# Padding the weight buffers and the halves of h in an encoder trunk, so that their SBUF addresses are staggered

## Chip, cores and metric

One core of one Trainium2 chip runs the whole program in a single launch. The metric is the device time of one execution in microseconds (us), lower is better. The kernel before takes 1731.49 us (median of 3 runs, 1730.62 to 1733.04).

## What is computed

A two-layer encoder trunk on x of 512 positions by 1024 channels, in float32. Cut to what matters:

```python
for l in range(DEPTH):                                   # 2 layers
    mod = jax.nn.silu(c) @ w_ada[l] + b_ada[l]           # shift, scale, gate, twice
    h = layer_norm(x) * (1.0 + scale1) + shift1
    proj = h @ w_in[l]                                   # 1024 x 7168: q, k, v of 3 groups, pooling, 2 gates
    att = ...                                            # dilated band attention, 3 groups, 8 heads of 64
    y_att = att.reshape(B, S, ATT_WIDTH) @ w_att_out[l]
    pooled = ...                                         # centred pooling, mixed per group, scaled
    y_pool = pooled @ w_pool_out[l]
    merged = jax.nn.sigmoid(gate_att) * y_att + jax.nn.sigmoid(gate_pool) * y_pool
    x = layer_norm(ALPHA * x + (1.0 + gate1) * (merged @ w_o[l]), ln1_g[l], ln1_b[l])
    h2 = layer_norm(x) * (1.0 + scale2) + shift2
    a_, b_ = jnp.split(h2 @ w_ffn_in[l], 2, axis=-1)     # 1024 x 5632
    x = layer_norm(ALPHA * x + (1.0 + gate2) * ((jax.nn.silu(a_) * b_) @ w_ffn_out[l]), ln2_g[l], ln2_b[l])
```

## The kernel before

Positions and channels are cut into tiles of 128. Every large product is done in three float32r matmuls: both factors are split into a rounded part (hi) and a remainder (lo), and `mm3` (L237) adds hi·hi, hi·lo and lo·hi into one PSUM bank (L239, L240, L241). `proj` (L243) calls it for the eight 128-channel steps of h: the stationary operand is a 128x128 slice of a weight tile, the moving operand 512 columns (all positions) of h.

The weights come as chunks of 128x1024 (512 KB) by DMA from the SP queue into `raw` buffers, and `split` (L197) makes hi and lo of each: ACT rounds, DVE or POOL subtracts. `prefetch` (L86) walks the list of chunks ahead of use; by the list, hi and lo go either into buffers of the tag `w` (8 of 4,096 bytes in each partition) or into buffers of the tag `g` (23 of 4,096 bytes), which also hold activations, attention operands and weight tiles that stay. The tag `h` has two buffers of 16,384 bytes: each is one half of h, four channel tiles with hi and lo of 512 positions each (`new_h`, L267). `h(k)` (L270) is tile k, a pair of 512-column rows.

The stages of a layer, in program order: `values` (L381, matmuls of L389, where h is stationary and a weight row moving), pooling, q and k with attention in between, `gates` and `merge` (the second matmul group there has pooled or attended tiles of `g` moving against `w`), then `tail` (L764) for the product with w_o; `ffn_in` (L864, the first tiles in two halves of 256 columns, some of them from `g`); and `tail` again for w_ffn_out. In `tail` the matmuls (L775) have 128 columns of a `g` tile stationary and a 512-column half of a weight row moving, from `w` for most and from `g` for resident weights; each weight row is used by six matmuls for each tile of positions.

A pool places its tags one after the other in a partition. In values of 4 bytes, the built program before has the eight `w` buffers 1,024 apart, the two halves of h behind them 4,096 apart, and all ten start 232 values past a multiple of 512; the `g` buffers start 56 past one. Weight slices start at multiples of 128 in their buffer. So the difference between a moving row of h and a stationary slice of `w` is always a multiple of 128; that between a moving row of `w` and a stationary slice of `g` is 48 (modulo 128), and that between a moving tile of `g` and a slice of `w` is 80 (modulo 128).

DMAs that the POOL engine issues (activations, rows of constants, small exchanges for attention) use a scratch area of SBUF, 16,384 bytes of each partition at address 0.

Of the kernel before, what the change touches and what calls it, by code (L numbers as in the profile page):

```python
# [13 lines left out]
F32R = mybir.dt.float32r  # L14
# [3 lines left out]
D = 1024  # L18
S = 512
# [9 lines left out]
P = 128  # L29
# [11 lines left out]
NW = 8  # L41
# [7 lines left out]
class Net:  # L49
# [38 lines left out]
    def prefetch(self, loads, splits, scales=None):  # L88
        n = len(self.plan)
        scales = max(splits, scales or splits)  # L90
        loads = max(loads, scales)
        info = lambda i: (self.plan[i] + (None,))[2]
        for i in range(min(n, self.pos + loads)):
            if i not in self.raws and i not in self.ready:
                self.raws[i] = self.chunk(self.plan[i][0])
        for i in range(min(n, self.pos + scales)):
            if i in self.raws and i not in self.scaled and info(i) is not None and info(i) >= 0:
                assert not self.ada
                self.scaled.add(i)
                self.nc.gpsimd.tensor_mul(self.raws[i], self.raws[i], self.gate[info(i)][0])  # L100
        for i in range(min(n, self.pos + splits)):
            if i not in self.ready:
                raw = self.raws.pop(i)
                if self.plan[i][1] == "w":
                    hi, lo = (self.t("w", [P, D], F32R, NW) for _ in range(2))
                else:
                    hi, lo = self.g([P, D], F32R), self.g([P, D], F32R)
                self.split(hi, lo, raw, info(i) == -1)
                self.ready[i] = (hi, lo)
# [155 lines left out]
        return r  # L265

    def new_h(self):  # L267
        self.hA = [self.t("h", [P, 4, 2, S], F32R, 2) for _ in range(2)]

    def h(self, k):  # L270
        return self.hA[k // 4][:, k % 4]
# [749 lines left out]

# [11 lines left out]
```

## Time and profile before

| what | value |
|---|---|
| median of 3 runs | 1731.49 us |
| lowest and highest run | 1730.62 and 1733.04 us |
| profiled execution, first to last instruction (span) | 1732.1 us |
| the same execution in the view of cores | 1732.1 us, mean granted TensorE clock 0.994 |
| TensorE (PE) busy | 1688.3 us, 97%, 8162 matmuls |
| DVE, ACT, POOL busy | 965.5, 658.7, 351.1 us |
| share of PE in the chain that ended last | 90% |

The page tells of one profiled execution. Of PE it says when a matmul starts; ends are modelled and overlap the next start, so the pace is read from starts. PEld is the load of the stationary operand, one for each matmul. A view of groups gives, behind the count, the busy time, the mean duration of one in ns, and the idle time in front of them with what ended it.

### The profile page before, as it was taken

The page shows a single profiled execution, that of the slowest core. Times are in us where ns is not written, and L with a number is a line of the kernel's source. Part 1 is how long each engine was busy: PE and PEld are TensorE (multiplying, and loading weights), DVE is VectorE, ACT ScalarE, POOL GpSimd, SP SyncE. Part 2 cuts the span into 40 slices and gives each one's busy share as a digit, 9 for nine tenths or more (in the row PEclk, how much of TensorE's full clock was granted, in tenths as well). Part 3 has the DMA queues.
Part 4 walks back from the last instruction along what each step waited for, and adds up shares of the span by engine and source line. Part 5 has one row for each costly group of instructions (what it writes and reads, how often), then busy time and mean ns, then how long its engine had stood idle before and what let it go on. Part 6 is the DMA issues. An engine that isn't in the chain of part 4 may idle for free.

```text
span 1732.1 us, 21129 instructions
## 1 busy us (share of the span) xinstructions
PE 1688.3 (97%) x8162; PEld 1384.0 (80%) x8162; DVE 965.5 (56%) x1628; ACT 658.7 (38%) x1110; POOL 351.1 (20%) x317
## 2 busy tenths in 40 slices
PE   7899999999989999999999999999999999999998
PEld 5687788888779888888878887878887888888886
DVE  8657677545685554333473676764367844333435
ACT  4246444633443222221352554446234422222212
POOL 4301221002340000255330021120032400004540
PEclk9999999999999999999999999999999999999999
DMA  7524444332532555332522254452325344322331
GB/s 273 203 73 166 157 136 138 109 113 81 195 110 96 190 195 176 111 108 96 184 110 79 83 173 134 143 162 86 98 98 182 110 146 146 97 98 97 106 138 49
DMA packets 63799, 227.20 MB, mean 131 GB/s; under 512 B 7681, under 2 KB 8097, under 8 KB 63698
## 3 DMA queue, kind: packets, MB, share of 16 engines
q1 hardware_dynamic: 55296, 199.25, 33.9%
q0 software_dynamic: 8400, 26.59, 4.8%
q8 instruction: 64, 1.05, 0.3%
q14 instruction: 37, 0.30, 0.1%
q10 hardware_dynamic: 2, 0.00, 0.0%
HBM read 217.28 MB, written 8.54 MB: 130 GB/s over the span
## 4 chain that ended last, share of the span: by engine, by line
PE 90%; DVE 6%; ACT 2%; issue 1%; DMA 0%; POOL 0%; DVEq 0%
PE mm L239 21%; PE mm L241 20%; PE mm L240 20%; PE mm L775 8%; PE pt L775 5%; PE s L775 4%; PE mm L607 2%; PE mm L389 1%; DVE raw L205 1%; PE pt L389 1%; PE s L542 1%; PE s L541 1%; PE pt L573 1%; DVE nt L260 1%; DVE rs L264 1%
## 5 line engine op out<-in xcount | busy, mean ns | idle before, releaser
L239 PE MATMUL mm<-h,w 128*128 128x512 f32 (+1 forms) x1440 | 560.6, 389 | 0.0
L241 PE MATMUL mm<-h,w 128*128 128x512 f32 (+1 forms) x1440 | 554.6, 385 | 0.0
L240 PE MATMUL mm<-h,w 128*128 128x512 f32 (+1 forms) x1440 | 553.7, 385 | 0.0
L199 DVE TENSOR_TENSOR w<-raw,w 128x1024 fp32r<-128x1024 f32 x238 | 309.8, 1316 | 188.5 <-ACT w L198 188.5
L198 ACT CAST w<-raw 128x1024 fp32r<-128x1024 f32 x254 | 259.8, 1044 | 168.4 <-PE mm L775 141.7
L239 PEld LDWEIGHTS mm<-h,w 128*128 128x128 f32 x1440 | 270.6, 188 | 57.0 <-issue 3.8
L241 PEld LDWEIGHTS mm<-h,w 128*128 128x128 f32 x1440 | 270.6, 188 | 55.4
L240 PEld LDWEIGHTS mm<-h,w 128*128 128x128 f32 x1440 | 270.8, 188 | 52.4
L100 POOL TENSOR_TENSOR raw<-raw,g 128x1024 f32<-128x1024 f32 x60 | 158.2, 2648 | 375.0 <-DMA raw<-w_ffn_out 221.4
L198 ACT CAST g<-g 128x512 fp32r<-128x512 f32 x76 | 47.2, 621 | 336.7 <-DVE g L871 217.0
L775 PE MATMUL mm<-w,g 128*128 128x512 f32 x600 | 147.2, 395 | 0.0
L871 DVE TENSOR_TENSOR g<-g,mm 128x512 f32<-128x512 f32 x42 | 28.9, 688 | 211.4 <-PE mm L241 198.8
L775 PEld LDWEIGHTS mm<-w,g 128*128 128x128 f32 x600 | 112.6, 188 | 27.1
L205 DVE SCALAR_TENSOR_TENSOR raw<-raw,silc 128x1024 f32<-128x1024 f32 x96 | 132.2, 1384 | 1.6 <-DMA raw<-w_ada 1.6
L199 DVE TENSOR_TENSOR g<-g,g 128x512 fp32r<-128x512 f32 x76 | 61.9, 815 | 70.8 <-ACT g L198 70.8
L775 PE MATMUL s<-w,g 128*128 128x512 f32 x300 | 78.9, 403 | 2.1 <-ACT w L198 1.3
L775 PE MATMUL pt<-w,g 128*128 128x512 f32 x300 | 76.3, 395 | 0.0
L775 PEld LDWEIGHTS s<-w,g 128*128 128x128 f32 x300 | 57.5, 193 | 17.1 <-ACT w L198 1.8
L775 PEld LDWEIGHTS pt<-w,g 128*128 128x128 f32 x300 | 56.4, 188 | 13.6
L232 POOL DMA_DIRECT2D dg<-gr x4 | 2.1, 536 | 290.2 <-DVE gr L230 290.2
L473 POOL CAST kp<-kp 64x640 fp32r<-64x640 f32 x8 | 10.9, 1368 | 235.0 <-ACT kp L465 235.0
L870 ACT ACTIVATE g<-mm 128x512 f32<-128x512 f32 x42 | 25.2, 600 | 84.6 <-PE mm L241 84.6
(229 smaller groups left out, 2085.6 us busy)
## 6 DMA issues: line engine op xcount, KB each, us to landing
raw<-w_in SPq DMA_DIRECT2D x112, 512.0 KB, 3.3
raw<-w_ada SPq DMA_DIRECT2D x96, 512.0 KB, 4.3
raw<-w_ffn_in SPq DMA_DIRECT2D x88, 512.0 KB, 3.3
raw<-w_ffn_out SPq DMA_DIRECT2D x44, 512.0 KB, 3.2
raw<-w_o SPq DMA_DIRECT2D x16, 512.0 KB, 4.2
xs<-g POOLq DMA_DIRECT2D x12, 512.0 KB, 2.9
g<-xs POOLq DMA_DIRECT2D x12, 512.0 KB, 5.9
g<-d POOLq DMA_DIRECT2D x16, 256.0 KB, 5.6
```

Source lines behind the costliest of these rows:

```text
L100: self.nc.gpsimd.tensor_mul(self.raws[i], self.raws[i], self.gate[info(i)][0])
L198: self.nc.scalar.copy(dst_hi, src)
L199: (self.nc.gpsimd if pool else self.nc.vector).tensor_sub(dst_lo, src, dst_hi.bitcast(F32))
L205: self.nc.vector.scalar_tensor_tensor(raw, raw, 1.0, self.silc, op0=ALU.mult, op1=ALU.mult, accum_out=self.mod[:, l, m : m + 1])
L239: mm(out, lhsT=whi, rhs=xhi, start=first, stop=False)
L240: mm(out, lhsT=whi, rhs=xlo, start=False, stop=False)
L241: mm(out, lhsT=wlo, rhs=xhi, start=False, stop=last)
L389: nc.tensor.matmul(pv[p, g], lhsT=hh[:, hi, tk], rhs=w[k][wi][:, c], start=k == 0 and i == 0, stop=k == KD - 1 and i == 2)
L607: nc.tensor.matmul(o, lhsT=v, rhs=rhs, start=b == 0, stop=b == 1)
L775: mm(acc[t][hf], lhsT=src[k][:, part, tk], rhs=wx[:, hf * S : hf * S + S], start=k == 0 and part == 0 and wi == 0, stop=k == K - 1 and par ...
L870: nc.scalar.activation(tmp[:, 0], pa, AF.Silu)
L871: nc.vector.tensor_mul(tmp[:, 1], tmp[:, 0], pb)
```

## The change

Every `w` buffer is 8 values (32 bytes) longer, and the program uses the first 1,024 of it as before. Every half of h is 64 values (256 bytes) longer, and the program uses the first 4,096. The scratch area for the DMAs of POOL goes from 16,384 to 8,192 bytes. Together the ten buffers take 768 bytes more of each partition.

```diff
@@ prefetch
-                    hi, lo = (self.t("w", [P, D], F32R, NW) for _ in range(2))
+                    hi, lo = (self.t("w", [P, D + 8], F32R, NW)[:, 0:D] for _ in range(2))
@@ new_h
-        self.hA = [self.t("h", [P, 4, 2, S], F32R, 2) for _ in range(2)]
+        self.hA = [
+            self.t("h", [P, 8 * S + 64], F32R, 2)[:, 0 : 8 * S].rearrange("p (k e s) -> p k e s", k=4, e=2)
+            for _ in range(2)
+        ]
@@ kernel
-    nc = bacc.Bacc("TRN2", target_bir_lowering=False, num_devices=1)
+    nc = bacc.Bacc("TRN2", target_bir_lowering=False, num_devices=1, dynamic_dma_scratch_size=8192)
```

No instruction is added, removed or moved on any engine: each engine's list is the same, line by line, but for addresses. In the built program of the change the `w` buffers start 232, 240, 248, ... 288 values past a multiple of 512, the halves of h 296 and 360 past one, the `g` buffers 56 past one as before. The difference between a moving row of h and a stationary slice of `w` now takes, modulo 128, the sixteen values 0, 8, 16, ... 120 instead of 0 alone, in nearly equal numbers, by which buffer a chunk happens to get; `w` moving against `g` takes 48, 56, ... 104 instead of 48; `g` moving against `w` takes 24, 32, 48, ... 80 instead of 80.

## Rows read from the trace of the kernel before

**Rows 1.** The page: span and busy time of the engines.
```profile
span 1732.1 us, 21129 instructions
PE 1688.3 (97%) x8162; PEld 1384.0 (80%) x8162; DVE 965.5 (56%) x1628; ACT 658.7 (38%) x1110; POOL 351.1 (20%) x317
PEclk9999999999999999999999999999999999999999
```
**Rows 2.** The page: shares of the chain that ended last, by engine.
```profile
PE 90%; DVE 6%; ACT 2%; issue 1%; DMA 0%; POOL 0%; DVEq 0%
```
**Rows 3.** Groups by shape (line, engine, operation, names, shapes, count | busy us, mean ns | idle before).
```profile
L239 PE MATMUL mm<-h,w 128*128 128x512 f32 x1376 | 542.5, 394 | 0.0
L241 PE MATMUL mm<-h,w 128*128 128x512 f32 x1376 | 536.5, 390 | 0.0
L240 PE MATMUL mm<-h,w 128*128 128x512 f32 x1376 | 535.6, 389 | 0.0
L775 PE MATMUL mm<-w,g 128*128 128x512 f32 x600 | 147.2, 395 | 0.0
L775 PE MATMUL s<-w,g 128*128 128x512 f32 x300 | 78.9, 403 | 2.1 <-ACT w L198 1.3 <-DVE w L199 0.7
L775 PE MATMUL pt<-w,g 128*128 128x512 f32 x300 | 76.3, 395 | 0.0
L239 PE MATMUL mm<-g,w 128*128 128x512 f32 x128 | 50.5, 395 | 0.0
L239 PE MATMUL pt<-h,w 128*128 128x256 f32 x64 | 18.7, 292 | 0.0
```
**Rows 4.** Timeline of PE near 300 us (start, duration, line): h against w.
```profile
299.82 0.39 PE L241 MATMUL mm<-h,w 128*128 128x512 f32 x1
...
302.54 0.39 PE L241 MATMUL mm<-h,w 128*128 128x512 f32 x1
```
**Rows 5.** Timeline of the weight loads near 300 us.
```profile
299.82 0.19 PEld L239 LDWEIGHTS mm<-h,w 128*128 128x128 f32 x1
300.05 0.19 PEld L240 LDWEIGHTS mm<-h,w 128*128 128x128 f32 x1
```
**Rows 6.** Timeline of PE near 382 us: g against w.
```profile
381.79 0.39 PE L241 MATMUL mm<-g,w 128*128 128x512 f32 x1
...
383.86 0.39 PE L241 MATMUL mm<-g,w 128*128 128x512 f32 x1
```
**Rows 7.** Timeline of PE near 1713 us, in the last tail.
```profile
1712.71 2.96 PE L775 MATMUL mm<-w,g 128*128 128x512 f32 x12
1715.51 1.54 PE L775 MATMUL mm<-g,g 128*128 128x512 f32 x6
1716.89 2.49 PE L775 MATMUL mm<-w,g 128*128 128x512 f32 x10
```
**Rows 8.** Timeline of PE near 530 us: 256 columns of h against w.
```profile
529.26 0.28 PE L240 MATMUL pt<-h,w 128*128 128x256 f32 x1
...
530.94 0.28 PE L239 MATMUL pt<-h,w 128*128 128x256 f32 x1
```
**Rows 9.** Timeline of PE near 540 us: 256 columns of h against g.
```profile
539.91 0.28 PE L239 MATMUL mm<-h,g 128*128 128x256 f32 x1
...
541.44 0.28 PE L240 MATMUL mm<-h,g 128*128 128x256 f32 x1
```
**Rows 10.** Timeline of PE near 1373 us: 256 columns of h against g.
```profile
1373.16 0.28 PE L241 MATMUL mm<-h,g 128*128 128x256 f32 x1
...
1374.97 0.28 PE L239 MATMUL mm<-h,g 128*128 128x256 f32 x1
```
**Rows 11.** DMA issues (engine, count, KB each, us to landing) and the software queue.
```profile
q0 software_dynamic: 8400, 26.59, 4.8%
xs<-g POOLq DMA_DIRECT2D x12, 512.0 KB, 2.9
g<-xs POOLq DMA_DIRECT2D x12, 512.0 KB, 5.9
g<-d POOLq DMA_DIRECT2D x16, 256.0 KB, 5.6
```
**Rows 12.** Waits of PE (who waited for whom: us in total, times, longest).
```profile
PE mm L389 <- ACT h L375: 11.8, 7, 2.4
PE s L280 <- ACT g L838: 6.1, 4, 2.8
PE pt L240 <- DVE h L853: 5.4, 2, 2.9
```

## The prediction, made before the changed kernel was run

> **What bounds the kernel now.** [...] The chain that ended last is PE for 90% of its length, with DMA and POOL at 0% [rows 2], and the longest waits of PE come to 11.8, 6.1 and 5.4 us in total [rows 12]. So the time is the number of matmuls times their pace, and the change can matter only through that pace: it adds and moves no instruction. Next come the groups by shape. Three lines, L239 to L241, hold 4,128 matmuls of 512 columns of h against a slice of `w`, with no idle time before them [rows 3]; in L775 another 1,200 have a row of `w` moving against a slice of `g` [rows 3].
>
> Their durations (389 to 403 ns) are no pace, since they overlap. The pace is read from starts in the timeline. Of h against `w`, twelve steps take 2.72 us, 226.7 ns each [rows 4]; in 256 columns, fourteen steps take 1.68 us, 120.0 ns each [rows 8]. The difference, 106.7 ns for 256 columns, makes 213.3 ns for 512, so 13.3 ns of each matmul do not grow with its width. The load of the next stationary slice starts with the matmul, at 299.82 in both views [rows 4, 5]: two reads of SBUF run side by side, and what they cost each other is the question here.
>
> Whether their addresses matter can be seen before the change, because the trace has other differences. With 80 (modulo 128), `g` against `w`, in the same three lines and the same order, nine steps take 2.07 us, 230.0 ns [rows 6]. With 48, `w` against `g` in L775, twelve take 2.80 us, 233.3 ns; just behind it the same line with both from `g`, difference 0, takes 1.38 us for six, 230.0 ns [rows 7]. In 256 columns, 48 (h against `g`) takes 1.53 us for 13 steps, 117.7 ns [rows 9], and in another place 1.81 us for 16 steps, 113.1 ns [rows 10], both below the 120.0 of difference 0. So the 13.3 ns become 16.7 (230.0 less 213.3) or 20.0 (233.3 less 213.3) in wide matmuls, and 11.0 or 6.4 (117.7 or 113.1 less 106.7) in narrow ones. The address pair goes with the pace, by a few ns, to both sides.
>
> **The change, part by part.** The times below are made against the profiled execution, 1732.1 us, which stands 0.6 us above the median of 1731.49; sums are added to the median.
>
> *h against `w`, 512 columns: 4,128 matmuls.* Their difference goes from 0 to sixteen values, only one of which is 0 and only two of which (48 and 80) are in this trace at all. I bound the mean pace from the nearest rows. Upper end: all at the 230.0 of `g` against `w`, the same lines, width and order, +3.3 ns, +13.6 us. Lower end: the 256-column rows, -2.3 ns (117.7 against 120.0), -9.5 us; the lowest narrow row would be -6.9 ns, -28.5 us. I take half of the upper end, +1.65 ns or +6.8 us: the wide rows are nearest in form, and both of them with another difference than 0 lie above 226.7; but some of the sixteen may be as good as 0, so not all of them pay. Besides, the difference now changes with each hi and lo buffer, so a run no longer has one fixed difference to settle at.
>
> *`w` against `g` in the tails: 1,200 matmuls.* They sit at the highest pace of the wide rows, 233.3, and keep their 48 in about one of eight. Bounds: -3.3 ns (the 230.0 of the same line with difference 0), -4.0 us; and 0. I take the middle, -2.0 us.
>
> *256 columns of h against `w`: 384 matmuls* (six groups of 64 like the one shown) [rows 3]. Bounds -2.3 and 0 ns; the middle, -0.4 us.
>
> *`g` against `w` (384, three groups of 128 like the one shown [rows 3]) and `values` (384 in L389).* Some of their differences change. They run between 226.7 and 233.3 already, so I take 0 and keep 2.5 us (3.3 ns times 768) to each side.
>
> *ACT and DVE write, DMA fills.* `raw` buffers, which the DMAs write, keep their size; hi and lo are written at starts that are multiples of 32 bytes as before. I cost this at 0: ACT and DVE are busy for 38% and 56% [rows 1]. If that cover went, PE would wait for h or w, as it does now for 5.4 us [rows 12].
>
> *Half the scratch.* The software queue moves 8,400 packets in the whole run, and its transfers land 2.9 to 5.9 us after their issue [rows 11]. The trace does not show how full the scratch is. Below: nothing can be gained. Above: if each of the 12 loads of x in `g<-xs` waited for one earlier landing, 12 times 5.9 us, 71 us, of which POOL and DMA have none on the chain now [rows 2]. The issuing engine is idle for four fifths of the time, and each load stands a whole tail ahead of its use, so I take 0, and up to 3 us in the range.
>
> Sum: 6.8 - 2.0 - 0.4 = +4.4 us, 1731.5 + 4.4 = 1735.9, forecast **1736 us**, 0.26% slower. About 0.2% (3.5 us) is what a measurement of this kernel can tell from no change.
>
> **Rivals.** *The staggered addresses read past each other (faster).* For: both narrow rows with difference 48 are below that with 0; half of the new differences are odd multiples of 8, of which no wide matmul of this trace has one, and the 13.3 ns that do not grow with the width are there to be won. Against: no wide row here is below 226.7 for long. It decides from the point where the mean of the sixteen is under 226.7. At -2.3 ns for 4,128 and -4.0 us in the tails it gives 1731.5 - 9.5 - 4.0 = 1718 us; at the lowest narrow row, 1731.5 - 28.5 - 4.0 = 1699. [...]
>
> *All sixteen cost what the tails cost (slower by more).* 233.3 for 4,128 matmuls: 6.6 ns each, +27.2 us, and the tails stay as they are: 1759 us. For: it is the widest sample of a difference other than 0. Against: the rows of `g` against `w` are at 230.0.
>
> *The address pair is not what sets the pace (no change).* The rows with other differences are also other places of the program with other operands, other PSUM banks and other order, and in L775 the pace with difference 0 (230.0) is that of `g` against `w`. Then padding does nothing: 1731 to 1732 us. [...]
>
> **How the numbers follow.** Chances: the forecast (a little slower, 1735 to 1748) 0.36; all at the tails' pace or above 1748 0.11; faster, 1718 or below and up to 1728, 0.35; nothing, 0.18. The first two make slower 0.47. The range goes from 1715 (the faster case at 1718, less the 2.5 us for the two small groups) to 1750 (13.6 + 2.5 + 3 us above the median: all at 230.0, the small groups and the scratch at their upper ends); the case at 1759 and the lowest narrow row, together under 2 in 10, are left out. The forecast's own range is 1735 to 1748.
>
> **What would show it.** In the profile after, the instruction counts, and the waits of PE, should stand as they are. The pace of h against `w`, read from starts, should differ from place to place, with some pairs of buffers at about 226.7 and others at 230 or more, mean near 228.3; the tails' rows should fall from 233.3 towards 231.7. If the mean of h against `w` is under 226.7, or single places show 220 or less, the forecast is wrong and the first rival right; if it is 226.7 everywhere, the third. If POOL's DMA issues take longer, or PE waits for h in the tails for more than the 5.4 us [rows 12], the scratch has a price that I put at 0.

## The result and the profile after

The changed kernel takes 1749.88 us (median of 4 runs, 1746.73 to 1752.90), the kernel before 1731.05 us in the same comparison: 18.8 us more, a ratio of 1.0101 with a 95% interval of 1.0083 to 1.0120. It is slower, 0.1 us inside the upper end of the range (1750; two of the four runs lie above it) and well above the 1736 that was forecast.

The page of the changed kernel, the lines that answer to [rows 1, 2]:

```profile
span 1751.1 us, 21129 instructions
PE 1706.1 (97%) x8162; PEld 1382.5 (79%) x8162; DVE 962.3 (55%) x1628; ACT 658.8 (38%) x1110; POOL 352.0 (20%) x317
PE 90%; DVE 6%; ACT 2%; issue 1%; DMA 0%; POOL 0%; DVEq 0%
```

The counts and the chain are as before; PE is busy 17.8 us longer, the other engines as long as before to within 3.2 us. The waits of PE in the changed kernel (us in total, times, longest), which answer to [rows 12]:

```profile
PE mm L392 <- ACT h L378: 10.1, 6, 2.4
PE s L283 <- ACT g L841: 6.5, 4, 3.0
PE pt L240 <- DVE h L856: 5.7, 2, 2.9
```

These three come to 22.3 us, those of [rows 12] to 23.3; all waits of PE in the view come to 37.2 us, before to 35.8. So waits hold at most 1.4 of the 18.8 us, and the time went into the matmuls themselves. The groups by shape, which answer to [rows 3] (lines below L273 have moved by 3):

```profile
L239 PE MATMUL mm<-h,w 128*128 128x512 f32 x1376 | 548.3, 398 | 0.0
L240 PE MATMUL mm<-h,w 128*128 128x512 f32 x1376 | 543.4, 395 | 0.0
L241 PE MATMUL mm<-h,w 128*128 128x512 f32 x1376 | 543.1, 395 | 0.0
L778 PE MATMUL mm<-w,g 128*128 128x512 f32 x600 | 146.3, 394 | 0.0
L778 PE MATMUL s<-w,g 128*128 128x512 f32 x300 | 77.3, 397 | 1.7 <-ACT w L198 1.0 <-DVE w L199 0.8
L778 PE MATMUL pt<-w,g 128*128 128x512 f32 x300 | 75.9, 394 | 0.0
```

The three groups of h against `w` have together 20.2 us more busy time, the three of the tails 2.9 us less. Starts say the same more exactly. Near 303 us of the changed kernel:

```profile
302.60 0.40 PE L240 MATMUL mm<-h,w 128*128 128x512 f32 x1
...
305.66 0.40 PE L241 MATMUL mm<-h,w 128*128 128x512 f32 x1
```

That is thirteen steps in 3.06 us, 235.4 ns each, where [rows 4] have 226.7. This is one of the slowest places; the mean is below. In the last tail, beside [rows 7]:

```profile
1728.96 5.74 PE L778 MATMUL mm<-w,g 128*128 128x512 f32 x24
1734.54 1.55 PE L778 MATMUL mm<-g,g 128*128 128x512 f32 x6
```

24 steps of `w` against `g` take 5.58 us, 232.5 ns, below the 233.3 of before. Over the whole trace the mean step of h against `w` (each start to the next one, 4,064 pairs with no step over 280 ns in either trace) goes from 227.5 to 232.6 ns, that of the tails from 233.3 to 231.7, that of `g` against `w` from 230.5 to 232.1. All steps of h against `w` together, longer ones with them, sum to 20.9 us more, those of the tails to 3.3 us less, `g` against `w` to 0.6 us more.

### The profile page after: what moved, and what is told of

The parts are those of the page before. It is cut to its first block, busy times and chain, and to the rows that moved or that the text cites. A ratio compares the mean times of both kernels' runs of the same rounds, so it can differ in the third digit from the quotient of the medians.

```text
span 1751.1 us, 21129 instructions
## 1 busy us (share of the span) xinstructions
PE 1706.1 (97%) x8162; PEld 1382.5 (79%) x8162; DVE 962.3 (55%) x1628; ACT 658.8 (38%) x1110; POOL 352.0 (20%) x317
## 4 chain that ended last, share of the span: by engine, by line
PE 90%; DVE 6%; ACT 2%; issue 1%; DMA 0%; POOL 0%; DVEq 0%
PE mm L239 21%; PE mm L240 21%; PE mm L241 21%; PE mm L778 8%; PE pt L778 4%; PE s L778 4%; PE mm L610 2%; PE mm L392 1%; DVE raw L205 1%; PE pt L392 1%; PE s L545 1%; PE s L544 1%; PE pt L576 1%; DVE nt L260 1%; DVE rs L264 1%
## 5 line engine op out<-in xcount | busy, mean ns | idle before, releaser
L239 PE MATMUL mm<-h,w 128*128 128x512 f32 (+1 forms) x1440 | 566.2, 393 | 0.0
L240 PE MATMUL mm<-h,w 128*128 128x512 f32 (+1 forms) x1440 | 561.4, 390 | 0.0
L241 PE MATMUL mm<-h,w 128*128 128x512 f32 (+1 forms) x1440 | 561.1, 390 | 0.0
L199 DVE TENSOR_TENSOR w<-raw,w 128x1024 fp32r<-128x1024 f32 x238 | 304.9, 1295 | 190.0 <-ACT w L198 190.0
```

The lines of the kernel that those rows point to most:

```text
L199: (self.nc.gpsimd if pool else self.nc.vector).tensor_sub(dst_lo, src, dst_hi.bitcast(F32))
L239: mm(out, lhsT=whi, rhs=xhi, start=first, stop=False)
L240: mm(out, lhsT=whi, rhs=xlo, start=False, stop=False)
L241: mm(out, lhsT=wlo, rhs=xhi, start=False, stop=last)
```

## The experiments

Two theories stood against each other from the start. **A:** each difference between the moving and the stationary address has its own price. **B:** a fixed difference settles at a good pace whatever it is, and a difference that changes from load to load does not. **C** was added for the first run: where an address stands for itself counts.

### b1: a table of differences, by itself

The model is left out. On loaded data, one big tile stands for h and one for w (each a multiple of 1,024 values long, so that the difference is the one set); 48 matmuls run for each setting of the differences of hi and lo, in the order of `mm3`, then 96 for each in the order of a tail. Cut to what matters:

```python
for hi, lo in [(0, 0), (8, 8), (16, 16), ..., (120, 120), (0, 8), (0, 64), (0, 16), (64, 72), (16, 80)]:
    for _ in range(2):
        for k in range(8):
            mm(out, lhsT=w[hi](k), rhs=h_hi(k), ...)
            mm(out, lhsT=w[hi](k), rhs=h_lo(k), ...)
            mm(out, lhsT=w[lo](k), rhs=h_hi(k), ...)
```

> Leaves the whole model out: 48 matmuls of 512 columns for each of 25 address settings in the order of mm3, then 96 for each of 16 settings in the order of the tail, on loaded data, nothing else running. Read is the mean spacing of starts. Theory A (every difference has its own price, fixed or not): with hi and lo at the same difference, 0 gives 226.7 ns and most of 8 to 120 give 230 to 235; the mean over the sixteen is near the 232.6 ns of the changed kernel. Theory B (a fixed difference settles, a changing one does not): each of the sixteen fixed differences settles near 226.7 to 229, and only the settings in which hi and lo differ (0 and 8, 0 and 64, 0 and 16) stand at 231 to 234. Theory C (the start relative to a 64-byte line counts, not the difference): moving and weights shifted together by 8 values is slow (231 or more), together by 16 or 64 as fast as 0. In the tail's order 48 gives 233.3 and 0 about 227 to 230 by A; by B all are alike.

The timeline of this run, the same two matmuls (number 24 and 45) of the settings 0, 8, 16, 48 and 64, of hi at 0 with lo at 16, and of 0 with both operands moved by 8 values:

```profile
16.48 0.39 PE L76 MATMUL b<-h,w 128*128 128x512 f32 x1
...
21.24 0.39 PE L76 MATMUL b<-h,w 128*128 128x512 f32 x1
...
27.53 0.39 PE L76 MATMUL b<-h,w 128*128 128x512 f32 x1
...
32.43 0.40 PE L76 MATMUL b<-h,w 128*128 128x512 f32 x1
...
38.62 0.39 PE L76 MATMUL b<-h,w 128*128 128x512 f32 x1
...
43.42 0.39 PE L76 MATMUL b<-h,w 128*128 128x512 f32 x1
...
83.36 0.39 PE L76 MATMUL b<-h,w 128*128 128x512 f32 x1
...
88.26 0.39 PE L76 MATMUL b<-h,w 128*128 128x512 f32 x1
...
105.60 0.39 PE L76 MATMUL b<-h,w 128*128 128x512 f32 x1
...
110.36 0.39 PE L76 MATMUL b<-h,w 128*128 128x512 f32 x1
...
216.80 0.39 PE L76 MATMUL b<-h,w 128*128 128x512 f32 x1
...
221.67 0.39 PE L76 MATMUL b<-h,w 128*128 128x512 f32 x1
...
249.90 0.39 PE L76 MATMUL b<-h,w 128*128 128x512 f32 x1
...
254.66 0.39 PE L76 MATMUL b<-h,w 128*128 128x512 f32 x1
```

Each pair is 21 steps apart: 4.76 us (226.7 ns) at 0, 4.90 (233.3) at 8, 4.80 (229) at 16, 4.90 (233.3) at 48, 4.76 (226.7) at 64, 4.87 (231.9) at hi 0 with lo 16, and 4.76 (226.7) with both moved. The whole table, mean step of the second half of each setting in ns:

| difference (values) | 0 | 8 | 16 | 24 | 32 | 40 | 48 | 56 |
|---|---|---|---|---|---|---|---|---|
| order of `mm3` | 226.7 | 233.3 | 229.0 | 233.5 | 233.1 | 234.1 | 233.3 | 233.4 |
| 64 values more | 226.7 | 233.2 | 229.0 | 233.4 | 233.1 | 234.1 | 233.3 | 233.4 |
| order of a tail | 226.7 | 233.3 | 228.9 | 233.4 | 233.3 | 234.3 | 233.3 | 233.3 |

A fixed difference sets the pace by itself, from 226.7 ns at 0 to 234.1 at 40: nothing else runs, and the two orders agree to 0.2 ns. In these steps of 8 it repeats after 64 values (256 bytes), which I had not thought of: I had taken 128. Of theory B one half falls, since fixed differences do not settle but stay where they are. Theory C falls, since moving both, by 8, 16, 64 or 232 values, changes nothing (tried at difference 0 alone, 226.7 ns). Of the settings with unlike hi and lo, 0 with 64 stands at 226.7, being equal modulo 64, and 0 with 8 at 231.1, between the two. But 0 with 16 stands at 231.3, above both 226.7 and 229.0: a mixture can cost more than either of its parts, and this half of theory B does not fall. The mean of the eight is 232.0 ns.

### e1: half the scratch alone

```diff
-    nc = bacc.Bacc("TRN2", target_bir_lowering=False, num_devices=1)
+    nc = bacc.Bacc("TRN2", target_bir_lowering=False, num_devices=1, dynamic_dma_scratch_size=8192)
```

> The kernel before with only the scratch area halved (8,192 bytes); all buffers keep their sizes and their differences. Theories A, B and C: 1731 us, within 0.2%, pace of h against w 227.5 ns as before. Rival (half the scratch costs): up to the whole 18.8 us, that is up to 1750 us, with waits of PE for h or of POOL for its DMAs.

1732.06 us against 1732.00, ratio 1.0001 (0.9992 to 1.0011). The scratch costs nothing that can be measured.

### e2 and e3: the two paddings one at a time

e2 leaves w as before, e3 leaves h as before; the scratch is halved in both.

```diff
 e2
-                    hi, lo = (self.t("w", [P, D + 8], F32R, NW)[:, 0:D] for _ in range(2))
+                    hi, lo = (self.t("w", [P, D], F32R, NW) for _ in range(2))
 e3
-            self.t("h", [P, 8 * S + 64], F32R, 2)[:, 0 : 8 * S].rearrange("p (k e s) -> p k e s", k=4, e=2)
+            self.t("h", [P, 4, 2, S], F32R, 2)
```

> The changed kernel without the padding of w: the first half of h at difference 0, the second at 64, hi and lo of a weight at the same difference. Theory A: half of the 4,128 matmuls of h against w at 231 ns, the other half at 227.5: +7 us, 1738 us. Theory B: a fixed difference of 64 settles, +0 to 2 us, 1731 to 1733. Rival (padding h costs for itself): +10 us or more.

> The changed kernel without the padding of h: w staggered by 8 values a buffer, both halves of h at the same place. Theories A and B: 232 to 233 ns for h against w as in the changed kernel, tails 231.7: 1748 to 1752 us. If the stagger of w is not the cause: 1731 to 1738 us.

e2: 1732.13 us, ratio 0.9994 (0.9984 to 1.0003). e3: 1749.85 us, ratio 1.0098 (1.0083 to 1.0113), the whole loss. Taken alone e2 speaks for B, and the number that A gave for it was wrong. The table tells why: the second half of h stands at 64, which costs what 0 costs (226.7 ns in both). The groups of e3 are those of the changed kernel to the tenth:

```profile
L239 PE MATMUL mm<-h,w 128*128 128x512 f32 x1376 | 548.3, 398 | 0.0
L240 PE MATMUL mm<-h,w 128*128 128x512 f32 x1376 | 543.4, 395 | 0.0
L241 PE MATMUL mm<-h,w 128*128 128x512 f32 x1376 | 543.1, 395 | 0.0
```

### e4 and e5: two whole kernels on which A and B differ most

e4 staggers w by 64 values a buffer instead of 8, so addresses differ from load to load as much as in the changed kernel, but all differences are multiples of 64. e5 is the kernel before with h alone moved by 8: one fixed difference.

```diff
 e4, against the changed kernel
-                    hi, lo = (self.t("w", [P, D + 8], F32R, NW)[:, 0:D] for _ in range(2))
+                    hi, lo = (self.t("w", [P, D + 64], F32R, NW)[:, 0:D] for _ in range(2))
 e5, against the kernel before
-        self.hA = [self.t("h", [P, 4, 2, S], F32R, 2) for _ in range(2)]
+        self.hA = [
+            self.t("h", [P, 8 * S + 64], F32R, 2)[:, 8 : 8 * S + 8].rearrange("p (k e s) -> p k e s", k=4, e=2)
+            for _ in range(2)
+        ]
```

> The changed kernel with w padded by 64 values a buffer in place of 8: sixteen staggered addresses as well, but every difference between h and w a multiple of 64. Theory A with a period of 64: the time of the kernel before, 1731 us within 0.3%. Theory B (a difference that changes from load to load is what costs): 1748 to 1752 us, as the changed kernel.

> The kernel before with h alone moved by 8 values (both halves; w not padded, scratch not halved): every difference between h and w is 8 modulo 64, fixed. Theory A: 4,128 matmuls from 227.5 to 233.3 ns, +24 us, and 0.6 us in values: 1755 us. Theory B: it settles, 1731 to 1735 us.

e4: 1732.77 us, ratio 1.0003 (0.9994 to 1.0012). e5: 1756.75 us, ratio 1.0139 (1.0123 to 1.0155), with a mean step of h against `w` of 233.3 ns. Both are as A had it. By e4 a change of address from load to load by multiples of 64 costs nothing that can be measured; its differences are all equal modulo 64, so it says nothing of mixtures. The timeline of e5 near 302 us, eleven steps in 2.56 us, 232.7 ns each, with starts rounded to 10 ns:

```profile
301.36 0.40 PE L240 MATMUL mm<-h,w 128*128 128x512 f32 x1
301.59 0.40 PE L241 MATMUL mm<-h,w 128*128 128x512 f32 x1
...
303.92 0.40 PE L239 MATMUL mm<-h,w 128*128 128x512 f32 x1
```

### e6: every difference a multiple of 64

If A is right, the kernel before has something to gain: its tails stand at 48 and `g` against `w` at 16 (modulo 64). 64 bytes put in ahead of w move w and h together.

```diff
-        nm = self.t("nm4", [P, NT], F32, 1)
+        nm = self.t("nm4", [P, NT + 16], F32, 1)[:, 0:NT]
```

> The kernel before with 64 bytes (16 values) put in ahead of w, so that w and h move together: h against w stays 0, and w against g, g against w and h against g go from 48 or 16 (modulo 64) to 0. Theory A: 1,200 matmuls of the tails from 233.3 to 226.7, -7.9 us, 384 of g against w from 230.5 to 227.5, -1.2 us, a little in values: 1722 us, 0.5% faster. If addresses matter only for h against w: 1731 us.

1723.31 us, ratio 0.9947 (0.9934 to 0.9960): faster than both kernels. Its last tail, and `g` against `w`, at the places of [rows 6, 7]:

```profile
1700.59 5.60 PE L775 MATMUL mm<-w,g 128*128 128x512 f32 x24
1706.03 1.52 PE L775 MATMUL mm<-g,g 128*128 128x512 f32 x6
1707.39 0.84 PE L775 MATMUL mm<-w,g 128*128 128x512 f32 x3
...
381.24 0.39 PE L241 MATMUL mm<-g,w 128*128 128x512 f32 x1
...
383.28 0.39 PE L241 MATMUL mm<-g,w 128*128 128x512 f32 x1
```

24 steps of the tail take 5.44 us (226.7 ns, before 233.3), and nine of `g` against `w` 2.04 us (226.7, before 230.0). The steps of the tails sum to 7.9 us less, as expected.

### b2: the table in steps of one value

As b1 with the order of `mm3` alone, for the differences 0 to 63, then with 256 columns, then with fewer stationary columns.

> Leaves the whole model out, as the table before: 48 matmuls in the order of mm3 for each difference 0, 1, 2 ... 63 values (hi and lo alike), then the same with 256 columns at 0, 8 ... 56, then with a stationary operand of 96, 64 and 32 columns at 0, 8, 16 and 40. Theory A with a period of 64 values: 0 gives 226.7 ns, the multiples of 8 repeat 233.3, 229.0, 233.4, 233.1, 234.1, 233.3, 233.4; what lies between is open, and a value below 226 would be a better place. If the two reads collide line by line of 4 values, the price goes in steps of 4 values (1 to 3 like 0 or 4) . If what exceeds 213.3 ns is the weight load's own reads, it shrinks with the columns loaded: 13.3 ns at 128 columns, about 10, 6.7 and 3.3 at 96, 64 and 32; if it is a fixed price of a matmul, it stays 13.3.

Mean step over 24 of each setting, in ns, for the single values 0 to 15: 226.7, 226.7, 233.3, 233.3, 228.3, 231.7, 231.1, 231.1, 233.3, 233.3, 231.9, 236.7, 233.3, 236.0, 230.8, 233.3. Only 0, 1, 31 and 34 stand at 226.7, none lower; the highest is 25 at 243. There is no better place than 0, and no step of 4 values is to be seen. With 256 columns the order is another. The timeline, the same 24 steps at difference 0 and at 48:

```profile
729.36 0.28 PE L78 MATMUL b<-h,w 128*128 128x256 f32 x1
...
732.24 0.28 PE L78 MATMUL b<-h,w 128*128 128x256 f32 x1
...
763.33 0.28 PE L78 MATMUL b<-h,w 128*128 128x256 f32 x1
...
766.05 0.28 PE L78 MATMUL b<-h,w 128*128 128x256 f32 x1
```

That is 2.88 us (120.0 ns a step) and 2.72 us (113.3). All eight:

| difference | 0 | 8 | 16 | 24 | 32 | 40 | 48 | 56 |
|---|---|---|---|---|---|---|---|---|
| 256 columns, ns | 120.0 | 116.7 | 117.8 | 120.0 | 118.6 | 117.3 | 113.3 | 118.3 |

0 and 24 are the worst there and 48 the best. With 96, 64 and 32 stationary columns difference 0 takes 230.0, 230.0 and 231.7, difference 40 takes 230.5, 226.7 and 230.5. So what exceeds 213.3 ns does not shrink in step with the columns loaded; that guess is wrong. Nor are the 13.3 ns a fixed part of each matmul, as the prediction read them: at the best place of each width the paces are 226.7 and 113.3, one twice the other, and nothing is left that does not grow with the width.

### b3: whose difference counts

Weight slices alternate between two differences, singly and in pairs, against one moving row.

> Leaves the whole model out: one moving row of 512 columns, and weight slices that alternate between two differences a and b, 64 matmuls for each of (0,8) (0,24) (0,40) (16,40) (0,16) (0,64) (8,72) (8,24); then the same in the order a a b b. If a matmul pays for the load of the next slice that runs beside it, the matmuls whose next slice has 8, 24 or 40 take 233 to 234 ns and those whose next has 0 take 226.7; if it pays for its own slice, the other way round; if only the mean is set and the parts carry over, both stand between, with a mean of 230.0 for (0,8). (0,64) stands at 226.7 and (8,72) at 233.3 in any case.

Alternating singly, the matmuls with their own slice at 0 and the next at 8 take 235.0, those with 8 and the next at 0 take 231.7; for 0 and 40 both take 230.0, for 0 and 24 231.8 and 231.5, for 0 and 16 both 230.0; 0 with 64 takes 226.7. 8 with 72 has a mean of 233.3, but its steps alternate between 231.9 and 234.7 though the two differences are equal modulo 64. The price does not go to one matmul of the pair, so whether it belongs to the load of the next slice or to the own one stays open. A mixture is often not the mean of its parts: 0 and 8 take 233.3 against 230.0, 0 and 16 take 230.0 against 227.9 and 231.2 in pairs, 16 and 40 take 230.0 against 231.6, which is less.

### e7: a forecast from the table

```diff
 e7, against the changed kernel
-                    hi, lo = (self.t("w", [P, D + 8], F32R, NW)[:, 0:D] for _ in range(2))
+                    hi, lo = (self.t("w", [P, D + 16], F32R, NW)[:, 0:D] for _ in range(2))
```

> The changed kernel with w padded by 16 values a buffer in place of 8. Theory A, by the table of the eight differences (226.7, 233.3, 228.9, 233.3, 232.3, 234.3, 233.3, 233.3 ns for 0, 8 ... 56 modulo 64): h against w now takes 0, 16, 32 and 48 alone, mean 230.3 ns, +2.8 to 3.6 ns for 4,128 matmuls, 11.6 to 14.9 us; the tails 230.3, -3.0 ns for 1,200, -3.6 us; the rest +1 us: 1740 to 1744 us. If any stagger of less than 64 costs the same: 1750 us.

1743.92 us, ratio 1.0071 (1.0054 to 1.0088), mean step of h against `w` 230.9 ns. The table, made without the model, forecasts the kernel to a few us. (The expectation has 232.3 for difference 32, where b1 has 233.1 to 233.4; with that its range moves up by about 1 us. The tails came to 231.6 ns, not 230.3.)

## Why the prediction was right and wrong

*Slower, and where.* Right: almost nothing but the pace of the matmuls changed, and the largest term was h against `w`. PE's waits stand to 1.4 us, the other engines' busy time to 3.2 us.

*The time.* That 1749.88 lies in the range is luck, and it lies where the chances had 0.11 (all at the tails' pace or above 1748), not in the forecast's own 1735 to 1748. The sum, +4.4 us, was a quarter of the 18.8. The upper end of the range was made of 13.6 us for h against `w`, 2.5 for the small groups and 3 for the scratch; measured were 20.9, some 0.7 and nothing, with 3.3 us gained in the tails. A bound that was too low was covered by allowances for things that did not happen.

*The size of that term.* Wrong by three times. The step that failed is "I take half of the upper end, +1.65 ns or +6.8 us". Measured: +5.1 ns (227.5 to 232.6), +20.9 us. Its upper end, 3.3 ns from `g` against `w` [rows 6], was no upper end: 80 is 16 modulo 64, and 16 is the second cheapest of the eight values at 228.9 to 229.0. The other wide row, the tails' 48 at 233.3 [rows 7], was the typical one, as five of the eight stand at 233.1 to 233.5. The halving rested on "some of the sixteen may be as good as 0": by the table two of the sixteen are, 0 and 64, and in the changed kernel not even these, as the part on changing differences shows.

*The lower end from narrow matmuls.* Also wrong, and the reason for leaning low. [rows 8 to 10] were read as a gain for 48 that wide matmuls might share. b2 shows that 256 columns have an order of their own, with 48 the best at 113.3 and 0 among the worst at 120.0, where 512 columns have 0 the best. The 13.3 ns "that do not grow with the width" came from [rows 4, 8], which compare 512 columns at their best difference with 256 at one of their worst.

*The tails.* The term, -2.0 us or -1.67 ns, was right in its pace: 233.3 to 231.7; with longer steps counted, -3.3 us. That the middle of two bounds met it was luck: the lower bound, 230.0 for difference 0, came from six steps of [rows 7] that stand between rows of another difference; in e6, where the rows around them are at 0 too, the same six take 1.36 us, 226.7 ns each. *256 columns of h against `w`*: -0.4 us was expected, and their steps sum to 0.4 us less; the mean step of those in the `mm` banks goes from 120.0 to 118.4. *`g` against `w` and `values`*: inside the 2.5 us kept for them. *Scratch, writes, DMAs*: 0, as e1 shows for the scratch and e4 (ratio 1.0003, with the scratch halved and `w` and `h` moved) for all three together. The wait for h that was named as a sign of a price went from 5.4 to 5.7 us, and is 5.4 in e1.

*The rivals.* The faster one is out: no difference of whole values brings 512 columns below 226.7 in b2. The "no change" one is out by b1, where 0 and 8 differ by 6.6 ns (226.7 and 233.3) with nothing else running. The one with all at the tails' pace, 1759 us, was nearest in its price for h against `w`, 233.3 against 232.6, and left out that the tails would gain.

*Whether a changing difference hurts for itself.* The prediction said that a run "no longer has one fixed difference to settle at", and put no number to it. A change by multiples of 64 costs nothing that can be measured (e4, ratio 1.0003), but unlike differences side by side can take longer than either alone (0 with 16 in b1: 231.3 ns, alone 226.7 and 229.0). The sign "some pairs of buffers at about 226.7" did not come: of the 172 groups of 24 matmuls that `proj` makes of h against `w`, the means of a step in the changed kernel lie between 230.8 and 235.2 ns (steps over 280 ns left out), those of the kernel before between 226.7 and 229.1. Five groups in a row begin at:

```profile
548.67 0.39 PE L239 MATMUL mm<-h,w 128*128 128x512 f32 x1
...
554.27 0.39 PE L239 MATMUL mm<-h,w 128*128 128x512 f32 x1
...
559.86 0.39 PE L239 MATMUL mm<-h,w 128*128 128x512 f32 x1
...
565.42 0.40 PE L239 MATMUL mm<-h,w 128*128 128x512 f32 x1
...
570.98 0.39 PE L239 MATMUL mm<-h,w 128*128 128x512 f32 x1
```

The steps to the next start are 233.3, 232.9, 231.7 and 231.7 ns a matmul, and nearly the same four come again and again until 690 us: the four pairs of the eight `w` buffers, in turn. In each pair lo has a difference 8 away from that of hi, so no group has a single difference. The size of this is an estimate. An equal mix of the eight table values, by the "nearly equal numbers" of the section on the change, would be 232.0 ns. But if hi always has the first buffer of a pair, as taking them in turn makes it, and stands in two of three matmuls, multiples of 16 weigh double and the table gives 231.5. The measured 232.6 is 0.6 to 1.1 ns above, 2.5 to 4.5 of the 20.9 us. Most of the loss is the price of the differences themselves; the rest is left to mixtures, for which b1 and b3 show prices without a rule.

Why the pace depends on the two addresses no run here shows. Shown is that for 512-column float32r matmuls a fixed difference of the two addresses sets the pace (b1: 226.7 ns at 0, 234.1 at 40, in steps of 8 values the same to 0.1 ns 64 values further on), and that moving both together by 8, 16, 64 or 232 values, at difference 0, does not change it (226.7 with both moved by 8).

## What to carry to other kernels

Where matmuls run back to back, read their pace from starts, and compare it between places whose operands lie differently in SBUF: here a few ns a matmul were 0.5% to 1.4% of the kernel. For 512-column float32r operands the best place of those tried is one where moving and stationary addresses differ by a multiple of 64 values (226.7 ns at 0 and 64 in b1); a stagger by 8 made it worse (232.6 ns, ratio 1.0101), and 64 bytes of filler in the right place gained 0.53% (e6). And a price taken from the one nearest row is a sample of one: when a change spreads over sixteen cases, measure the table first, which took one run, and with it the mixtures that the kernel will run.

## What the runs showed of the hardware that was not expected

The pace repeats after 64 values of 4 bytes (226.7 at 0 and 64, 233.3 and 233.2 at 8 and 72). The best place for 512 columns is one of the two worst of eight for 256 (226.7 and 120.0 at 0; 233.3 and 113.3 at 48). Two differences in turn can take longer than either alone (hi at 0 with lo at 16: 231.3, alone 226.7 and 229.0). No difference of 64 brings 512 columns below 226.7, and loading a quarter of the stationary columns does not either (231.7 ns at difference 0 with 32 columns); what sets that floor is open.
